# Mixer C's weight chunks: low parts made by accumulating transfers, high passes first, other hand-out rules in the planner

## The chip, the core and the metric

One core of one Trainium2 chip runs the whole program. The metric is the device time of one execution in microseconds (us), the median of the runs shown. TensorE (PE) multiplies, PEld is its weight load, VectorE is DVE, ScalarE is ACT, GpSimd is POOL, and SyncE (SP) issues most transfers from and to the memory off the core (HBM).

## What is computed

Two layers of an encoder over 512 tokens of 1024 channels, in float32. Each layer normalises and modulates its input, projects it once, runs three token mixers on the projections, and merges them by gates:

```python
for l in range(DEPTH):                                   # 2
    shift, scale, gate = jnp.split(c_act @ w_ada[l] + b_ada[l], 3, axis=-1)
    h = rms_norm(x, norm_w[l]) * (1.0 + scale) + shift
    (qa, ka, va, ga, qb, kb, vb, gb, xc, zc, bc, cc, dtf, dtb, mg) = split(h @ w_in[l])
    ya = mixer_a(qa, ka, va, ...) * silu(ga)             # attention, 8 heads
    yb = mixer_b(qb, kb, vb, ...) * silu(gb)             # dilated window attention, 12 heads
    yc = mixer_c(xc, zc, bc, cc, dtf, dtb, ...)          # two-way state space scan, 8 heads
    g_a, g_b, g_c = split(sigmoid(mg + b_gate[l]))
    merged = g_a * (ya @ w_proj_a[l]) + g_b * (yb @ w_proj_b[l]) + g_c * (yc @ w_proj_c[l])
    x = x + gate * (merged @ w_out[l])
```

## The kernel before

**Products.** Every float32 product is made of three passes in a reduced float32 format: an operand is split into a high part (rounded to that format) and a low part (the operand less its high part), and PE adds high·high, high·low and low·high. Weights come as chunks of 128 rows by 1024 columns (512 KB) from the tensor `wch`. `chunk` (line 527) loads one into a `wraw` buffer by a transfer issued from SP, rounds it into a `whi` buffer on ACT, and subtracts on DVE into a `wlo` buffer (line 535); there are three buffers of each. `mm` (line 549) walks a chunk's row blocks k and for each calls `mm_k` (line 539): two passes with the high block, one with the low block, before it goes to the next k. A projection of 8 row blocks (`proj`, line 559) is 24 matmuls of 512 columns.

**The order of work.** The program is first only recorded: each call on an engine becomes an operation with its tiles (`Rec.record`, line 228). A list scheduler (`schedule`, line 306) then plays the machine through with costs written in the code, takes at each moment the ready operation of the lowest priority number per engine, hands out tile buffers as it goes, and issues all in the order found. So an engine's queue order is fixed before the run, and an instruction in it waits in line behind those ahead of it. What steers the order: `AHEAD` (line 464) moves a chunk's loading and splitting that many operations ahead of its use; `RESERVE` (line 457) says how many buffers of a kind must stay free when an operation takes one out of turn (kinds not named there are never given out of turn); `patience` (line 218) and `wait` (line 219) are thresholds in nanoseconds and in shares of an operation's cost, for an operation whose port is taken by the other of DVE and POOL, and for giving way to urgent operations. Some operations are recorded for either of two engines, and the planner chooses.

**A layer.** `record` (line 1369) goes through mixer A, mixer B and mixer C, then the projection of C's branch, then the output projection `out` (line 1309), which for the first layer runs over into the next layer's normalisation. Work without a mixer of its own is kept in a list `fill` and is let in by `pump` at set places. In mixer C (`mixer_c`, line 1172) these are the 8 projections of branch A (`branch_steps`, line 1279), and of branch B the 8 gates (`gate_step`, line 1266) and 8 projections: 16 fill steps, let in after the heads (`PLAN["c"]`). So while mixer C is recorded, `chunk` is called 26 times in a layer: 12 of mixer C's own, 4 for branch A's projection, 8 for branch B's gates and 2 for its projection. A head of mixer C (`ssd_head`, line 1224) is four pairs of scans on DVE over rows in PSUM, sums and products of these on POOL or DVE, a split into parts on ACT and POOL or DVE, and 8 matmuls. Ahead of the heads `steps` (line 1092) makes the step sizes by some 40 small operations on DVE, one after the other, and behind them `tok_rms` (line 739) makes the norm that the branch needs.

**Where the stages lie in the profiled run** (us from the start): start of layer 0 until 82; its mixer A until 200 and mixer B until about 365; entry to mixer C 365 to 380, mixer C 380 to 545, its norm 545 to 563; branch C and output 563 to 643; turn to layer 1 643 to 680. Layer 1: mixer A until 835, mixer B until about 1003, mixer C 1003 to 1172, its norm until 1185, the rest until 1283.

Of the kernel before, what the change touches and what calls it, by code (L numbers as in the profile page):

```python
# [7 lines left out]
F32 = mybir.dt.float32  # L8
F32R = mybir.dt.float32r
I32 = mybir.dt.int32  # L10
AF = mybir.ActivationFunctionType
ALU = mybir.AluOpType
# [195 lines left out]
class Rec:  # L208
# [6 lines left out]
    hold = None  # L215
    urgent = False
    margin = 200
    patience = 0
    wait = 0.4

    def tile(self, tag, shape, dt=F32, psum=False):
        return V(Tl(tag, shape, dt, psum))
# [5 lines left out]
    def record(self, alts):  # L228
        op = Op()
        op.i = len(self.ops)  # L230
        op.prio = op.i + self.boost
        op.alts = {}
        op.dma = 0
        op.urgent = self.urgent and alts[0][1] != "dma_start"
        for eng, meth, args, kw in alts:
            kw = dict(kw)
            if meth == "matmul":
                kw["lhsT"], kw["rhs"] = args[1], args[2]
            out = kw.get("out", args[0] if args else None)
            writes = [out] if isinstance(out, V) else []  # L240
            if isinstance(kw.get("accum_out"), V):
                writes.append(kw["accum_out"])
            reads = [a for a in args[1:] if isinstance(a, V)] + \
                    [v for k, v in kw.items() if isinstance(v, V) and k not in ("out", "accum_out")]
            n = out.n if isinstance(out, V) else 1
            ptr = sum(1 for v in reads if v.n == 1 and n > 1)
            if meth == "dma_start":
                v = out if isinstance(out, V) else reads[0]
                op.dma = v.n * v.p * 4
                inside = all(isinstance(z, V) and not z.t.tag.startswith("dram") for z in (out, *reads))  # L250
                op.slow = 2 if inside and reads else 1
                c = (600 if eng == "sync" else 950, 0, False)
            elif eng == "tensor":
                c = cost_pe(meth, kw, args) + (False,)
            elif eng == "vector":
                if meth == "tensor_reduce":
                    n = reads[0].n
                c = cost_dve(meth, out, reads, ptr, "accum_out" in kw, n)
            elif eng == "scalar":
                c = cost_act(meth, out, reads, ptr, "accum_out" in kw, n)  # L260
            else:
                c = cost_pool(meth, out, reads, ptr, n)
            if meth == "matmul":
                kw.pop("lhsT"), kw.pop("rhs")
            op.alts[ENG[eng]] = (c[0], eng, meth, args, kw, c[1], c[2])
        deps = {}
        pe = eng == "tensor"
        for v in reads:
            for o, box, w in v.t.log:
                if w and self.meet(box, v.box):  # L270
                    deps[o] = 0
        for v in writes:
            if pe and v.t.psum and v.t.lastpe is not None:
                deps.setdefault(v.t.lastpe, 0)
            for o, box, w in v.t.log:
                if o is not op and self.meet(box, v.box) and not (pe and "PE" in o.alts):
                    deps[o] = 0
        for v in writes:
            if pe and v.t.psum:
                v.t.lastpe = op  # L280
            v.t.log = [e for e in v.t.log if not self.inside(e[1], v.box)] + [(op, v.box, True)]
        for v in reads:
            v.t.log.append((op, v.box, False))
        op.tiles = list({id(v.t): v.t for v in reads + writes}.values())
        for t in op.tiles:
            if t.left == 0:
                t.seq = len(self.tags.setdefault(t.tag, []))
                self.tags[t.tag].append(t)
            t.left += 1
        deps.pop(op, None)  # L290
        if meth == "dma_start" and self.hold is not None:
            deps.setdefault(self.hold, -2000)
        op.deps = deps
        op.succ = []
        self.ops.append(op)
        return op
# [157 lines left out]

class Kernel:
    SLOTS = {"wraw": 3, "whi": 3, "wlo": 3, "h": 16, "xs": 7, "gate": 3, "merged": 8, "tmp": 6, "P": 3, "bias": 1, "u4": 12, "q": 4, "s1": 32, "sm": 8, "dt": 2, "wa": 1}
    RESERVE = {"u4": 5, "tmp": 2, "sm": 3, "s1": 9, "ps_mm": 1, "ps_tp": 0, "wraw": 0, "q": 1, "ps_pv": 3}
    BYTES = {"wraw": 4096, "whi": 4096, "wlo": 4096, "u4": 4096, "P": 3072, "bias": 10240, "s1": 32, "sm": 256, "dt": 256,
             "dtr": 256, "dt96": 384}
    START = ("mm", "mm", "sc", "sc", "pv", "pv")  # L460
    POOLADA = ()
    ADAPE = (8, 9, 10)
    POOLLO = ()
    AHEAD = 1114
    WA = "wraw"
    START_W = (2, 3, 4, 5, 6, 6, 6, 6)
    URGENT, URGENT_ROWS = 2, False
    ROWS = ("sc", "sc")
    SOON = 100
    ADATAGS = ("whi", "wlo")  # L470
    PLAN = {"a": 5, "c": (5, 1, 1, 2, 2, 0, 4, 1)}
    BANKS = {"mm": 2, "sc": 2, "tp": 2, "pv": 2}

    def __init__(self, nc, tc, A, depth=DEPTH, dbg=None):
# [52 lines left out]
    def chunk(self, l, j, tags=("wraw", "whi", "wlo"), ahead=None, pool=False):  # L527
        nc = self.nc
        b, self.rec.boost = self.rec.boost, self.rec.boost - (self.AHEAD if ahead is None else ahead)
        raw = self.t(tags[0], [128, 1024])  # L530
        nc.sync.dma_start(raw, self.A["wch"][l, j])
        hi = self.t(tags[1], [128, 1024], F32R)
        nc.scalar.copy(hi, raw)
        lo = self.t(tags[2], [128, 1024], F32R)
        self.sub(lo, raw, hi.bitcast(F32), pool)
        self.rec.boost = b
        return hi, lo

# [8 lines left out]
        nc.tensor.matmul(ps, lo[:, c], xh, start=False, stop=(k == nk - 1), **kw)  # L547

    def mm(self, ps, w, c0, nk, xs):
        for k in range(nk):  # L550
            self.mm_k(ps, w, c0, k, nk, xs)

    def soon(self, f):

# [617 lines left out]
    def mixer_c(self, l):  # L1172
# [7 lines left out]
        for g in range(2):  # L1180
# [10 lines left out]
            for ti in range(2):  # L1191
# [4 lines left out]
                for s in range(2):  # L1196
                    po.append(self.ssd_head(2 * ct + s, s, X, cb, R, d8))
                    self.pump(self.PLAN["c"][2 * ct + s])
                y = self.gather_heads(po[0], po[1], False)
# [63 lines left out]
        return o  # L1263


    def gate_step(self, l, br, n):

        m = 8 * br + n
        ps = self.proj(l, CH_MG + m)
        if br == 0:  # L1270
            g = self.t("merged", [128, 512])
            self.merged.append(g)
        else:
            g = self.t("gate", [128, 512])
        self.soon(lambda: self.nc.scalar.activation(g, ps, AF.Tanh, scale=0.5,
                                                    bias=self.vec[l][:, V_BGATE + m:V_BGATE + m + 1]))
        return g

    def branch_steps(self, l, br, ys, gates=None):

        nk = len(ys)
        per = 8 // nk
        st = {}

        def step(n):
            nc = self.nc
            g = gates[n] if gates else self.gate_step(l, br, n)
            if n % per == 0:
                st["w"] = self.chunk(l, (CH_PA, CH_PB, CH_PC)[br] + n // per)
            p = self.ps("mm")  # L1290
            self.mm(p, st["w"], (n % per) * nk * 128, nk, lambda k: (ys[k][:, 0], ys[k][:, 1]))
            self.soon(lambda: nc.vector.scalar_tensor_tensor(g, g, 1.0, p, op0=ALU.add, op1=ALU.mult))
            if br:
                a = (self.merged[n], self.merged[n], g)
                self.rec.either(("vector", "tensor_add", a, {}), ("gpsimd", "tensor_add", a, {}))

        return [lambda n=n: step(n) for n in range(8)]
# [70 lines left out]

    def record(self):
        self.early = {}  # L1370
        self.xd = [self.dram([128, 512]) for _ in range(8)]
        self.setup()
        for l in range(self.depth):
            if l == 0:
# [22 lines left out]
                    self.early[l, z] = pss[z]  # L1397
                self.bias_vd = self.bias_rows(*self.bias_loads())
                self.setup2()
            self.bg = [(l, o) for o in range(16, 24)] + ([(l + 1, o) for o in range(16)] if l + 1 < self.depth else [])  # L1400
            self.merged = []
            n0 = self.PLAN["a"]
            self.fill = [lambda n=n: self.gate_step(l, 0, n) for n in range(n0)]
            ya = self.mixer_a(l)
            self.pump(8)
            yb = [self.mixer_b(l, jj) for jj in range(2)]
            st0 = self.branch_steps(l, 0, ya, self.merged)
            if n0 < 8:
                self.fill = [lambda n=n: self.gate_step(l, 0, n) for n in range(n0, 8)]
                self.pump(8)  # L1410
            self.fill = st0 + self.branch_steps(l, 1, yb)
            yc = self.mixer_c(l)
            self.pump(16)
            self.tick(24)
            self.fill = self.branch_steps(l, 2, yc)
            self.pump(8)
            self.out(l)

    def prepare(self):
# [2 lines left out]
    def build(self):  # L1422
        from contextlib import ExitStack
        nc, tc, rec = self.real_nc, self.tc, self.rec
        self.record()
        order = rec.schedule(self.RESERVE)
        self.order = order
# [149 lines left out]
```

## Time and profile before

| | before |
|---|---|
| median of 3 runs | 1284.81 us (1283.31 to 1287.2) |
| the profiled execution's own time | 1284.8 us |
| its span, first to last instruction | 1282.9 us |
| PE busy | 1229.2 us (96%), 6288 matmuls |
| DVE busy | 1018.6 us (79%) |
| ACT, POOL busy | 668.5 us (52%), 227.2 us (18%) |
| granted TensorE clock, mean | 0.989 |

Matmuls overlap in the profile: a matmul of 512 columns stands as some 0.39 us long while the next begins 0.23 us after it. So PE's busy time in a stretch tells when PE had nothing in flight, and the granted clock tells where it ran at half its speed; a difference of either from full is time in which PE could have done more. The other engines' busy times can be read as they stand. Every operation is issued from one helper line (L452), so groups are told apart by their tiles: `ps_mm<-h,wlo` is a projection's low pass, `wlo<-wraw,whi` the making of a chunk's low part.

### The profile page before, as it was taken

The page shows a single profiled execution, that of the slowest core. Times are in us where ns is not written, and L with a number is a line of the kernel's source. Part 1 is how long each engine was busy: PE and PEld are TensorE (multiplying, and loading weights), DVE is VectorE, ACT ScalarE, POOL GpSimd, SP SyncE. Part 2 cuts the span into 40 slices and gives each one's busy share as a digit, 9 for nine tenths or more (in the row PEclk, how much of TensorE's full clock was granted, in tenths as well). Part 3 has the DMA queues.
Part 4 walks back from the last instruction along what each step waited for, and adds up shares of the span by engine and source line. Part 5 has one row for each costly group of instructions (what it writes and reads, how often), then busy time and mean ns, then how long its engine had stood idle before and what let it go on. Part 6 is the DMA issues. An engine that isn't in the chain of part 4 may idle for free.

```text
span 1282.9 us, 17593 instructions
## 1 busy us (share of the span) xinstructions
PE 1229.2 (96%) x6288; PEld 1009.2 (79%) x6288; DVE 1018.6 (79%) x1876; ACT 668.5 (52%) x1138; POOL 227.2 (18%) x230
## 2 busy tenths in 40 slices
PE   6999999999989999999989999999999899999998
PEld 5778888788768777778887888887888777777887
DVE  7869977888799999964685889486787999998542
ACT  3447764665554555433344667556665454644320
POOL 0122110210024425300002121001101232442000
PEclk9999999999989999999989999999999998999999
DMA  9643215655312222333643331263342122222341
GB/s 356 212 119 114 66 55 170 179 168 191 89 50 66 66 66 83 99 106 124 213 132 90 108 99 34 83 187 109 95 138 75 53 80 66 66 82 83 123 148 58
DMA packets 49237, 144.32 MB, mean 112 GB/s; under 512 B 7254, under 2 KB 9814, under 8 KB 49150
## 3 DMA queue, kind: packets, MB, share of 16 engines
q1 hardware_dynamic: 49054, 143.07, 35.9%
q8 instruction: 50, 0.82, 0.3%
q14 instruction: 37, 0.30, 0.1%
q0 software_dynamic: 96, 0.13, 0.0%
HBM read 124.74 MB, written 4.27 MB: 101 GB/s over the span
## 4 chain that ended last, share of the span: by engine, by line
PE 76%; DVE 11%; DMA 6%; ACT 3%; issue 2%; SPq 1%; POOL 0%; DVEq 0%; ACTq 0%; POOLq 0%
PE ps_mm L452 55%; PE ps_sc L452 8%; PE ps_tp L452 7%; PE ps_pv L452 7%; DVE wlo L452 3%; DMA wraw<-in_wada 2%; DMA u<-u 2%; DVE u L452 2%; DVE xs L452 1%; DVE tmp L452 1%; DVE P L452 1%; ACT whi L452 1%; DVE q L452 1%; DMA wraw<-in_wch 1%; SPq L452 1%
## 5 line engine op out<-in xcount | busy, mean ns | idle before, releaser
L452 PE MATMUL ps_mm<-h,whi 128*128 128x512 f32 x1824 | 593.3, 396 | 4.3 <-ACT gate L452 3.9
L452 PEld LDWEIGHTS ps_mm<-h,whi 128*128 128x128 f32 x1824 | 340.0, 189 | 79.4 <-ACT gate L452 8.6
L452 PE MATMUL ps_mm<-h,wlo 128*128 128x512 f32 x912 | 359.8, 395 | 0.0
L452 ACT CAST whi<-wraw 128x1024 fp32r<-128x1024 f32 x157 | 164.8, 1051 | 197.7 <-PE ps_mm L452 186.3
L452 DVE TENSOR_TENSOR wlo<-wraw,whi 128x1024 fp32r<-128x1024 f32 x157 | 200.7, 1279 | 71.9 <-ACT whi L452 70.1
L452 PEld LDWEIGHTS ps_mm<-h,wlo 128*128 128x128 f32 x912 | 172.0, 189 | 35.6
L452 PE MATMUL ps_mm<-u,whi 128*128 128x512 f32 (+1 forms) x592 | 177.1, 379 | 16.2 <-DVE merged L452 15.3
L452 PEld LDWEIGHTS ps_mm<-u,whi 128*128 128x128 f32 x592 | 109.5, 192 | 38.5 <-DVE merged L452 17.3
L452 PE MATMUL ps_mm<-u,wlo 128*128 128x512 f32 (+1 forms) x296 | 111.0, 375 | 0.0
L452 PE MATMUL ps_pv<-u,u 128*128 128x256 f32 (+2 forms) x640 | 105.7, 291 | 4.1 <-ACT gate L452 2.8
L452 POOL TENSOR_SCALAR P<-P,s 128x512 f32<-128x512 f32 (+1 forms) x59 | 52.1, 887 | 319.0 <-DVE s L452 251.5
L452 DVE TENSOR_TENSOR u<-ps_tp,u 128x512 fp32r<-128x512 f32 (+2 forms) x174 | 82.7, 489 | 25.8 <-ACT u L452 24.5
L452 DVE TENSOR_TENSOR_SCAN P<-ps_sc,bias 128x512 f32<-128x512 f32 (+3 forms) x128 | 97.6, 803 | 1.6 <-PE ps_sc L452 1.4
L452 ACT CAST u<-ps_tp 128x512 fp32r<-128x512 f32 (+2 forms) x174 | 72.5, 428 | 49.5 <-PE ps_tp L452 44.9
L452 PEld LDWEIGHTS ps_pv<-u,u 128*128 128x128 f32 (+1 forms) x640 | 81.2, 173 | 15.7 <-ACT gate L452 3.0
L452 PE MATMUL ps_sc<-u,q 128*128 128x256 f32 (+1 forms) x320 | 82.9, 361 | 3.4 <-DMA u<-u 2.7
L452 PE MATMUL ps_tp<-const,P 128*128 128x128 f32 x448 | 68.9, 274 | 1.3 <-DVE sm L452 0.7
L452 ACT ACTIVATE bias<-const,dt 128x128 f32<-128x128 f32 x102 | 39.1, 400 | 54.8 <-DVE P L452 50.6
L452 PEld LDWEIGHTS ps_tp<-const,P 128*128 128x128 f32 x448 | 52.9, 140 | 16.4 <-issue 5.6
L452 PEld LDWEIGHTS ps_mm<-u,wlo 128*128 128x128 f32 x296 | 56.8, 192 | 9.8
L452 PEld LDWEIGHTS ps_sc<-u,q 128*128 128x128 f32 x320 | 51.6, 189 | 15.0 <-DMA u<-u 4.1
L452 POOL TENSOR_TENSOR tmp<-tmp,tmp 128x512 fp32r<-128x512 f32 (+1 forms) x15 | 20.6, 1375 | 215.1 <-ACT tmp L452 215.1
(168 smaller groups left out, 1811.2 us busy)
## 6 DMA issues: line engine op xcount, KB each, us to landing
wraw<-in_wch SPq DMA_DIRECT2D x168, 512.0 KB, 3.6
wraw<-in_wada SPq DMA_DIRECT2D x32, 512.0 KB, 3.5
u<-u SPq DMA_DIRECT2D x28, 256.0 KB, 3.7
merged<-in_xT SPq DMA_DIRECT2D x16, 256.0 KB, 3.3
whi<-in_wada SPq DMA_DIRECT2D x8, 512.0 KB, 7.0
wlo<-in_wada SPq DMA_DIRECT2D x8, 512.0 KB, 7.1
u<-u SPq DMA_DIRECT2D x64, 64.0 KB, 2.1
tmp<-xs SPq DMA_DIRECT2D x40, 64.0 KB, 2.7
```

Source lines behind the costliest of these rows:

```text
L452: getattr(getattr(nc, eng), meth)(*[get(a) for a in args], **{k: get(v) for k, v in kw.items()})
```

## The change

1. In `chunk`, while `self.adds` is set and the buffer is of the kind `wlo`: ACT writes the negative of the rounded chunk into `wlo` (an activation with scale -1), POOL issues a transfer that adds the same chunk from HBM onto it, and ACT makes `whi` after that. The subtraction on DVE goes. `self.adds` is set only while mixer C is recorded (`ADDS[0]`): 26 chunks in a layer, 52 in all; the other 4 places are off.
2. The planner counts an accumulating transfer at twice the bytes (`op.slow = 2`).
3. `mm` makes all high passes of a chunk's blocks first and then all low passes. `mm_k` is left for the callers that use it directly (the start and the turn between the layers).
4. `RESERVE`: u4 5 to 2, sm 3 to 2, ps_mm 1 to 0, ps_pv 3 to 1, gate and xs newly named with 1 and 2 (all looser); ps_tp 0 to 1, q 1 to 2 (tighter). `AHEAD` 1114 to 800, `patience` 0 to 300, `wait` 0.4 to 0.2.
5. `PLAN["g"]` is 0, so the list of gates `gc` stays empty, and `pump(24)` finds the same 16 steps as before.

```diff
@@ Rec
-    patience = 0
-    wait = 0.4
+    patience = 300
+    wait = 0.2
@@ record
-                op.slow = 2 if inside and reads else 1
+                op.slow = 2 if inside and reads or "accum_op" in kw else 1
@@ Kernel
-    RESERVE = {"u4": 5, "tmp": 2, "sm": 3, "s1": 9, "ps_mm": 1, "ps_tp": 0, "wraw": 0, "q": 1, "ps_pv": 3}
+    RESERVE = {"u4": 2, "tmp": 2, "sm": 2, "s1": 9, "ps_mm": 0, "ps_tp": 1, "wraw": 0, "q": 2, "ps_pv": 1, "gate": 1, "xs": 2}
-    AHEAD = 1114
+    AHEAD = 800
+    ADDS = (True, False, False, False, False)
@@ chunk
         hi = self.t(tags[1], [128, 1024], F32R)
-        nc.scalar.copy(hi, raw)
         lo = self.t(tags[2], [128, 1024], F32R)
-        self.sub(lo, raw, hi.bitcast(F32), pool)
+        if tags[2] == "wlo" and self.adds:
+            nc.scalar.activation(lo, raw, AF.Copy, scale=-1.0)
+            nc.gpsimd.dma_start(lo, self.A["wch"][l, j], accum_op=ALU.add)
+            nc.scalar.copy(hi, raw)
+        else:
+            nc.scalar.copy(hi, raw)
+            self.sub(lo, raw, hi.bitcast(F32), pool)
@@ mm
         for k in range(nk):
-            self.mm_k(ps, w, c0, k, nk, xs)
+            for z, x in enumerate(xs(k)):
+                nc.tensor.matmul(ps, hi[:, c[k]], x, start=(k == 0 and z == 0), stop=False)
+        for k in range(nk):
+            nc.tensor.matmul(ps, lo[:, c[k]], xs(k)[0], start=False, stop=(k == nk - 1))
@@ record of a layer
+            self.adds = self.ADDS[0]
             yc = self.mixer_c(l)
-            self.pump(16)
+            self.pump(24)
             self.tick(24)
+            self.adds = self.ADDS[1]
```

## Rows read from the trace of the kernel before

**Rows 1.** The page's first two parts: engines' shares, and the span in 40 slices.
```profile
PE 1229.2 (96%) x6288; PEld 1009.2 (79%) x6288; DVE 1018.6 (79%) x1876; ACT 668.5 (52%) x1138; POOL 227.2 (18%) x230
DVE  7869977888799999964685889486787999998542
PEclk9999999999989999999989999999999998999999
...
GB/s 356 212 119 114 66 55 170 179 168 191 89 50 66 66 66 83 99 106 124 213 132 90 108 99 34 83 187 109 95 138 75 53 80 66 66 82 83 123 148 58
```
**Rows 2.** Table by stretch: us, busy (count) of five engines, PEclk, DMA share, GB/s.
```profile
82.00:200.00 118.00, 117.83 (x640) 97.67 (x640) 102.96 (x191) 77.61 (x153) 23.08 (x22) 1.00 0.30 91
245.00:335.00 90.00, 89.02 (x527) 73.45 (x526) 75.87 (x175) 59.05 (x103) 11.24 (x9) 1.00 0.51 156
...
680.00:835.00 155.00, 152.25 (x809) 125.23 (x808) 117.42 (x203) 95.86 (x181) 25.61 (x28) 1.00 0.28 86
870.00:960.00 90.00, 89.41 (x532) 75.04 (x531) 66.10 (x153) 58.46 (x101) 10.28 (x10) 1.00 0.39 110
```
**Rows 3.** The same table, the six stretches around the two mixers C.
```profile
365.00:380.00 15.00, 9.83 (x59) 8.12 (x59) 14.87 (x37) 7.21 (x14) 2.33 (x3) 0.89 0.23 70
380.00:545.00 165.00, 159.31 (x684) 125.96 (x683) 158.83 (x230) 83.09 (x133) 64.03 (x70) 0.99 0.24 74
545.00:563.00 18.00, 16.22 (x69) 13.08 (x70) 11.00 (x25) 5.08 (x9) 0.00 (x0) 0.91 0.19 58
...
1003.00:1005.00 2.00, 1.05 (x5) 0.55 (x3) 2.00 (x4) 0.27 (x1) 0.00 (x0) 1.00 0.02 2
1005.00:1172.00 167.00, 157.46 (x666) 124.18 (x667) 157.96 (x236) 84.97 (x137) 63.07 (x57) 0.97 0.23 73
1172.00:1185.00 13.00, 11.14 (x55) 8.78 (x54) 10.67 (x24) 5.28 (x8) 0.00 (x0) 1.00 0.28 81
```
**Rows 4.** Groups by shape, DVE, 380 to 545: count | busy us, mean ns | idle before.
```profile
L452 DVE TENSOR_TENSOR wlo<-wraw,whi 128x1024 fp32r<-128x1024 f32 x23 | 32.4, 1413 | 0.3
L452 DVE TENSOR_TENSOR_SCAN P<-ps_sc,bias 128x512 f32<-128x512 f32 x16 | 19.2, 1198 | 0.0
...
L452 DVE TENSOR_SCALAR xs<-tmp,const 128x512 f32<-128x512 f32 x5 | 3.5, 700 | 0.0
```
**Rows 5.** The page's part 5: a chunk's parts, and projections' low passes on PE.
```profile
L452 PE MATMUL ps_mm<-h,wlo 128*128 128x512 f32 x912 | 359.8, 395 | 0.0
L452 ACT CAST whi<-wraw 128x1024 fp32r<-128x1024 f32 x157 | 164.8, 1051 | 197.7 <-PE ps_mm L452 186.3
L452 DVE TENSOR_TENSOR wlo<-wraw,whi 128x1024 fp32r<-128x1024 f32 x157 | 200.7, 1279 | 71.9 <-ACT whi L452 70.1
```
**Rows 6.** Timelines of DVE and PE at the entries: start, us, [idle before].
```profile
373.14 1.23 DVE L452 TENSOR_TENSOR wlo<-wraw,whi 128x1024 fp32r<-128x1024 f32 x1
...
376.68 1.28 DVE L452 SCALAR_TENSOR_TENSOR merged<-merged,ps_mm 128x512 f32<-128x512 f32 x2
...
377.42 0.79 PE L452 MATMUL ps_mm<-u,whi 128*128 128x512 f32 x1 [5.17 <-DVE merged L452]
...
1006.88 0.50 PE L452 MATMUL ps_mm<-u,whi 128*128 128x512 f32 x1 [2.83 <-DVE merged L452]
```
**Rows 7.** Chain that ended last: one stretch of projections, and behind layer 1's mixer C.
```profile
435.40 5.68 PE ps_mm L452 x25
...
1170.93 1.06 ACT whi L452
1172.01 1.22 DVE wlo L452
1173.27 0.71 DVE tmp L452
```
**Rows 8.** The page's part 6, transfers by issue: KB each, median us to landing.
```profile
wraw<-in_wch SPq DMA_DIRECT2D x168, 512.0 KB, 3.6
whi<-in_wada SPq DMA_DIRECT2D x8, 512.0 KB, 7.0
const<-in_ident POOLq DMA_DIRECT2D x1, 64.0 KB, 3.6
```
**Rows 9.** POOL's timeline at the start: start, us, one issue of a transfer.
```profile
1.27 0.76 POOL L452 DMA_DIRECT2D const<-in_vec  x1 [0.83 <-POOLq L1569]
```

More of the change, by code (lines that the diff above doesn't have):

```diff
@@ L470 @@
     ADATAGS = ("whi", "wlo")
-    PLAN = {"a": 5, "c": (5, 1, 1, 2, 2, 0, 4, 1)}
+    ADDS = (True, False, False, False, False)
+    PLAN = {"a": 5, "c": (5, 1, 1, 2, 2, 0, 4, 1), "g": 0}
     BANKS = {"mm": 2, "sc": 2, "tp": 2, "pv": 2}
@@ L549, in mm @@
     def mm(self, ps, w, c0, nk, xs):
+        nc = self.nc
+        hi, lo = w
+        c = [slice(c0 + k * 128, c0 + k * 128 + 128) for k in range(nk)]
         for k in range(nk):
-            self.mm_k(ps, w, c0, k, nk, xs)
+            for z, x in enumerate(xs(k)):
+                nc.tensor.matmul(ps, hi[:, c[k]], x, start=(k == 0 and z == 0), stop=False)
+        for k in range(nk):
+            nc.tensor.matmul(ps, lo[:, c[k]], xs(k)[0], start=False, stop=(k == nk - 1))
     def soon(self, f):
@@ L1263, in ssd_head, with gate_step @@
         return o
-    def gate_step(self, l, br, n):
+    def gate_step(self, l, br, n, tag="gate"):
         m = 8 * br + n
@@ L1273, in gate_step @@
         else:
-            g = self.t("gate", [128, 512])
+            g = self.t(tag, [128, 512])
         self.soon(lambda: self.nc.scalar.activation(g, ps, AF.Tanh, scale=0.5,
@@ L1286, in step @@
             nc = self.nc
-            g = gates[n] if gates else self.gate_step(l, br, n)
+            g = gates[n] if gates and n < len(gates) else self.gate_step(l, br, n)
             if n % per == 0:
@@ L1370, in record @@
         self.early = {}
+        self.adds = False
         self.xd = [self.dram([128, 512]) for _ in range(8)]
@@ L1399, in record @@
                 self.setup2()
+            self.adds = self.ADDS[3]
             self.bg = [(l, o) for o in range(16, 24)] + ([(l + 1, o) for o in range(16)] if l + 1 < self.depth else [])
@@ L1405, in record @@
             self.pump(8)
+            self.adds = self.ADDS[4]
             yb = [self.mixer_b(l, jj) for jj in range(2)]
@@ L1410, in record @@
                 self.pump(8)
+            gc = []
             self.fill = st0 + self.branch_steps(l, 1, yb)
+            self.fill += [lambda n=n: gc.append(self.gate_step(l, 2, n, "xs")) for n in range(self.PLAN["g"])]
+            self.adds = self.ADDS[0]
             yc = self.mixer_c(l)
-            self.pump(16)
+            self.pump(24)
             self.tick(24)
-            self.fill = self.branch_steps(l, 2, yc)
+            self.adds = self.ADDS[1]
+            self.fill = self.branch_steps(l, 2, yc, gc)
             self.pump(8)
+            self.adds = self.ADDS[2]
             self.out(l)
```

## Prediction

> **What bounds the kernel now.** I read the page's first two parts, then a table of busy times by stretch, then the groups of the stretch that stood out, and last the timeline where PE waits. PE is busy 96% of the span, so at first sight PE is the bound everywhere and a change on DVE can bring nothing [rows 1]. The slices tell more: DVE stands at 9 in two places, the two mixers C, and the granted clock drops from 9 to 8 near their ends [rows 1].
>
> The table by stretch makes it exact. In the mixers A and B of both layers PE idles 0.17 of 118 us, 0.98 of 90, 2.75 of 155 and 0.59 of 90, at full clock, with DVE busy 87%, 84%, 76% and 73% [rows 2]. That is 4.5 us of 453, or 1.0%: PE is the bound there, and a DVE at up to 87% does not hold it up. In the two mixers C DVE is busy 158.83 of 165 us and 157.96 of 167, or 96% and 95%, and PE idles 5.69 and 9.54 us [rows 3]. At the entry to layer 0's mixer C DVE is busy 14.87 of 15 us and PE idles 5.17 [rows 3]. So around the mixers C both are near full, DVE more so, and PE loses time to it.
>
> What is lost there: PE's idle time in the six stretches is 5.17 + 5.69 + 1.78 + 0.95 + 9.54 + 1.86 = 25.0 us [rows 3]. To it comes the clock. The granted share is 0.89 of 15 us, 0.99 of 165, 0.91 of 18 and 0.97 of 167, so 1.65 + 1.65 + 1.62 + 5.01 = 9.9 us of full-speed work is missing [rows 3]; each drop to the lower level, 1.2 instead of 2.4 GHz, follows a wait of PE. Together 34.9 us. More than that this change cannot win around mixer C.
>
> **The subtraction that goes.** 26 chunks per layer leave DVE. One subtraction takes 1.28 us in the mean over the kernel [rows 5] and 1.41 us in layer 0's mixer C [rows 4]; it is the largest group of DVE there, with 32.4 us for the 23 that fall into the stretch [rows 4]. 26 x 1.28 = 33 us a layer. DVE falls from 158.8 to about 126 us. If the stretch shrinks to some 156 us, that is 81%, which lies between the 73% and 87% at which PE was not held up [rows 2]. So DVE stops being the bound, and PE is next.
>
> **What stays lost.** (a) PE's own small waits at the rate of the other stages: 1.0% of the 380 us of the six stretches, 3.8 us [rows 2, 3]. (b) The norm behind mixer C is a chain of small dependent steps, in which PE lost 1.78 + 1.62 + 1.86 = 5.3 us [rows 3]. In the chain of layer 1 one subtraction of 1.22 us stands ahead of it on DVE [rows 7]; without one in each layer 2.8 us stay. (c) At the entries PE waits for DVE to empty a PSUM bank, 5.17 and 2.83 us [rows 6]. In the longer wait DVE works through its queue, of which one subtraction is only 1.23 us [rows 6]; the rest are the small operations of `steps` and others. With the clock of the first entry (1.65) 9.65 us are lost; I keep half, 4.8, since the queue ahead is shorter but the serial steps remain. 3.8 + 2.8 + 4.8 = 11.4 stay, and 34.9 - 11.4 = 23.5 us are won.
>
> **What is added.** ACT gets one more pass of 1.05 us per chunk [rows 5], 27 us a layer, and stands then at 83 + 27 = 110 of some 156 us (70%) [rows 3]; the same ACT also turns conv and gate outputs over, but at 70% it hides that. The high part is ready one pass later, and is loaded well ahead: PE waited 0.0 us ahead of the low passes [rows 5]. If that cover were gone, each chunk would cost up to 1.05 us.
>
> POOL gets 26 issues a layer. Nearest row: 0.76 us for an issue from POOL [rows 9]; 20 us, so POOL goes from 64 to 84 of 156 us [rows 3]. Each issue waits for ACT's negation, and behind it on POOL are the sums and products of the heads' scans, on which the heads' matmuls wait. Bounds: nothing, if the planner places the issue after the negation, to 26 x 1.05 = 27 us a layer, if POOL stands through one whole ACT pass each time and nothing else is ready. I take 1 us a layer, near the lower end, since POOL idles 101 of 165 us now [rows 3]. Together 2.
>
> The transfer itself: no row shows one that accumulates. A plain 512 KB chunk from SP lands after 3.6 us, under the load of the start after 7.0, a 64 KB one from POOL after 3.6 [rows 8]. Bounds 3.6 and, at the planner's factor of two on the longest, 14 us; I take 8, twice the plain one and a little for the load: 26 chunks of 0.52 MB are 13.6 MB a layer, 27 at twice their bytes; with the 12 MB that 74 GB/s move in 165 us [rows 3] that is 39 MB in 156 us, or 250 GB/s, 70% of the 356 seen in the first slice [rows 1]. So no lasting queue of transfers forms, but it is no longer a quiet stretch. SP's own queue gets nothing new; its loads wait for a free `wraw`, which ACT's second pass now frees instead of DVE.
>
> **High passes first.** The low part is wanted only after 16 of a chunk's 24 matmuls. A matmul takes 5.68 / 25 = 0.227 us [rows 7], so 3.6 us later: nearly half of the landing is hidden by that alone, the rest by loading ahead. The number of matmuls and weight loads is the same. What it costs: the last block's operand is wanted 7 matmuls sooner (15th instead of 22nd), at most 1.6 us where it is fresh. That is so only at the first output chunk of a layer; I take half, 0.8, twice, 1.6 us.
>
> **The planner's other numbers** (`RESERVE`, `AHEAD`, `patience`, `wait`) reorder all stages and no row prices them. The nearest measure is how far two orders of the same code differ: mixer A loses 0.17 of 118 us in one layer and 2.75 of 155 in the other [rows 2], 0.1% against 1.8%. 1.7% of the 453 us of these stages is 7.7 us, to either side; I take 0, as neither sign has a reason.
>
> **Sum.** 23.5 - 2 - 1.6 = 19.9 us. The profiled execution took 1284.8 us with a span of 1282.9, and is at the median of the runs (1284.81), so no further shift is due: 1284.8 - 19.9 = **1265 us**, 1.5% faster. Its own range: all 34.9 won and 4 of the 7.7, 1246; the 7.7 against it and 6 more for POOL, 1279.
>
> **A rule against it.** DVE's single-input elementwise form in this stretch is only five instructions of 3.5 us in all [rows 4]. The Trainium skill, SBUF — State Buffer, SBUF: two separate sides, says that a transfer issued from GpSimd has its descriptors written by GpSimd, and that a DVE instruction that takes both port pairs locks it out until it ends, so that the transfer looks blocked. By that rule five landings of 26 would come under 1 us later; the sum stays, and it adds to the chance of the second rival.
>
> **The rivals.** *No change:* the heads' own chain, scans on DVE, sums on POOL, split on ACT, matmuls, is the bound by its length, and PE waits as before; 1281 to 1288, say 1285. For it: ACT and POOL wait much for DVE's scans. Against: DVE has no gaps, its groups show 0.0 to 0.3 us idle [rows 4], so it lacks time, not input. 0.12.
>
> *The accumulating transfer lands late:* slower. A low buffer is held from the negation to its last low pass: 1.05 + 0.76 + landing + 8 x 0.227 = landing + 3.6 us. Three buffers serve 26 chunks in 165 us if this is under 3 x 6.35 = 19 us. So the point is a landing of 15.4 us; beyond it PE waits for chunks. At 18 us: 26 x 21.6 / 3 = 187 us, 22 more a layer, 1329 us. Against it: every 512 KB landing seen, 7.0 at most [rows 8]. Starved descriptors would be its cause. 0.09.
>
> *POOL's queue stands:* slower. POOL has 165 - 84 = 81 us to spare, so 3.1 us of standing per issue. At 4 us each POOL takes 64 + 26 x 4.76 = 188 us, 23 more a layer, 1331. Against it: the planner sees the negation's end before it places the issue. 0.09.
>
> **How the numbers follow.** Forecast 0.70, no change 0.12, late transfer 0.09, POOL 0.09. What a measurement can tell is 0.3%, 3.9 us: 1281 to 1288.7 is the same. Of the forecast's 0.70 about 0.02 falls there, and of the no-change rival's 0.12 about 0.03 on the faster side and 0.01 on the slower. Faster 0.71, same 0.10, slower 0.19. The range goes from the forecast's best end, 1246, over no change to 1288; 0.16 to 0.18 of the slower cases and a little below stay out.
>
> **What would show it.** Right: DVE in mixer C's stretch at 75 to 85%, no `wlo<-wraw,whi` there; the stretches from the entry to the norm's end shorter by 8 to 13 us in each layer, other stages within some us; the drops of the clock after the entries fewer; landings of the accumulating transfers of 4 to 9 us, and none named as what PE waits for. Wrong: PE's low passes waiting for a transfer or POOL; POOL's waits for ACT grown by over 80 us a layer; gains or losses that lie in the mixers A and B, which would make the planner's numbers the cause.

## The result, and the profile after

| | before | after |
|---|---|---|
| median | 1285.12 us (1283.31 to 1287.2) | 1262.58 us (1261.5 to 1268.03) |
| the profiled execution's own time | 1284.8 us | 1262.41 us |
| its span | 1282.9 us | 1260.6 us |
| granted TensorE clock, mean | 0.989 | 0.996 |

Both kernels ran on the same chip, four times each. The time after is 0.9833 of the time before, 95% interval 0.9801 to 0.9865: 22.5 us faster, where 19.9 were forecast.

The page of after: shares of the engines, the slices of DVE, POOL and the granted clock, and the groups and transfers of a low part (count | busy us, mean ns | idle before; KB and median us to landing):

```profile
PE 1222.3 (97%) x6288; PEld 1006.8 (80%) x6288; DVE 962.0 (76%) x1747; ACT 726.8 (58%) x1202; POOL 374.8 (30%) x347
...
DVE  7869966888698979864685899586767999897442
...
POOL 0033310020136858611014221001002385682110
PEclk9999999999999999999999999999999999999999
...
L452 POOL DMA_DIRECT2D wlo<-in_wch x52 | 46.2, 889 | 172.9 <-ACT wlo L452 153.3
...
wraw<-in_wch SPq DMA_DIRECT2D x168, 512.0 KB, 3.8
wlo<-in_wch POOLq DMA_DIRECT2D x52, 512.0 KB, 6.5
```

The clock's three eights of [rows 1] are gone (they stood at the entry to layer 0's mixer C, at the turn and at the end of layer 1's mixer C). But DVE still reaches 9 in slices of both mixers C, and POOL, busy 64.03 of 165 us in layer 0's mixer C before [rows 3], has slices of 5 to 8 in both. DVE has 129 instructions fewer. Only 52 of these are the subtractions, worth 52 x 1.28 = 67 us [rows 5]; the other 77 went to other engines in the new plan: POOL has 117 instructions more, 52 of them the issues, and ACT has 64 more, 52 of them the negations, which leaves 65 + 12. For all this DVE's busy time fell by 56.6 us only: what stayed on DVE became longer.

The table by stretch of after (us, busy (count) of PE, PEld, DVE, ACT, POOL, then the granted clock, DMA share, GB/s): entry to layer 0's mixer C, the mixer, its norm; the turn; the end of layer 1's mixer B, its mixer C, its norm. They answer to [rows 3].

```profile
365.00:377.00 12.00, 11.98 (x84) 10.08 (x83) 11.45 (x37) 8.83 (x22) 6.62 (x7) 1.00 0.73 154
377.00:530.00 153.00, 147.28 (x639) 117.43 (x639) 137.00 (x187) 102.96 (x158) 112.63 (x104) 0.99 0.63 141
530.00:550.00 20.00, 20.00 (x96) 16.58 (x95) 14.73 (x29) 8.83 (x12) 1.28 (x1) 1.00 0.25 79
630.00:670.00 40.00, 37.67 (x298) 36.04 (x297) 27.66 (x67) 18.50 (x35) 5.99 (x7) 1.00 0.33 106
...
945.00:986.00 41.00, 38.95 (x228) 31.73 (x227) 33.59 (x103) 28.40 (x61) 11.85 (x12) 0.96 0.53 117
986.00:1144.00 158.00, 150.04 (x669) 119.86 (x667) 145.66 (x192) 105.80 (x165) 106.52 (x103) 1.00 0.62 138
1144.00:1162.00 18.00, 17.82 (x84) 14.20 (x83) 14.32 (x29) 8.46 (x12) 0.00 (x0) 1.00 0.27 87
```

And the turn of before, which [rows 3] leave out:

```profile
643.00:680.00 37.00, 31.56 (x247) 31.36 (x248) 26.79 (x70) 15.15 (x28) 0.00 (x0) 0.91 0.36 114
```

Counted as in the prediction (PE's idle time plus the missing share of the clock), the stretches from the entry to the norm lost 34.9 us before. Now they lose 0.02 + (5.72 + 1.53) + 0 + 7.96 + 0.18 = 15.4 us: 19.5 won. The turn lost 5.44 + 3.33 = 8.8 and loses 2.3, 6.4 more won. Against that the end of layer 1's mixer B now loses 2.05 + 1.64 = 3.7 us, where before PE was busy 43.00 of 43 us (960 to 1003). These three make 22.2 of the 22.4 us between the two profiled executions; smaller shifts at the start and in layer 1's mixer A cancel within about 1.5 us.

What PE waits for after in layer 0's mixer C, then the longest wait in layer 1's (us in total, times, longest us), and what POOL waits for in the two:

```profile
PE ps_pv L452 <- ACT u L452: 3.5, 2, 2.4
PE ps_mm L452 <- ACT gate L452: 1.2, 3, 0.5
PE ps_pv L452 <- DVE u L452: 0.9, 1, 0.9
```
```profile
PE ps_tp L452 <- DVE xs L452: 3.1, 1, 3.1
```
```profile
POOL wlo L452 <- ACT wlo L452: 19.1, 12, 5.4
```
```profile
POOL wlo L452 <- ACT wlo L452: 34.8, 12, 7.8
```

No transfer is named for PE. In layer 0 what is late now is mostly the operand of the heads' own matmuls (`ps_pv`), split by ACT and DVE: the chain of the first rival, behind the forecast's bound. In layer 1 the longest single wait is for a result of DVE, `xs`.

### The profile page after: what moved, and what is told of

It is laid out like the page before. It is cut to its first block, busy times and chain, and to the rows that moved or that the text cites. A ratio compares the mean times of both kernels' runs of the same rounds, so it can differ in the third digit from the quotient of the medians.

```text
span 1260.6 us, 17709 instructions
## 1 busy us (share of the span) xinstructions
PE 1222.3 (97%) x6288; PEld 1006.8 (80%) x6288; DVE 962.0 (76%) x1747; ACT 726.8 (58%) x1202; POOL 374.8 (30%) x347
## 5 line engine op out<-in xcount | busy, mean ns | idle before, releaser
L452 PE MATMUL ps_mm<-h,whi 128*128 128x512 f32 x1824 | 476.6, 396 | 5.3 <-ACT gate L452 3.5
L452 PE MATMUL ps_mm<-h,wlo 128*128 128x512 f32 x912 | 244.2, 393 | 0.0
L452 DVE TENSOR_TENSOR wlo<-wraw,whi 128x1024 fp32r<-128x1024 f32 x105 | 136.9, 1305 | 79.0 <-PE ps_mm L452 47.9
L452 PE MATMUL ps_mm<-u,whi 128*128 128x512 f32 (+1 forms) x592 | 141.2, 375 | 0.3 <-ACT gate L452 0.2
L452 PEld LDWEIGHTS ps_mm<-u,whi 128*128 128x128 f32 x592 | 104.2, 188 | 20.6 <-ACT gate L452 0.6
L452 DVE TENSOR_TENSOR u<-ps_tp,u 128x512 fp32r<-128x512 f32 (+2 forms) x174 | 83.2, 490 | 21.4 <-ACT u L452 20.6
L452 POOL DMA_DIRECT2D wlo<-in_wch x52 | 46.2, 889 | 172.9 <-ACT wlo L452 153.3
L452 POOL TENSOR_TENSOR tmp<-tmp,tmp 128x512 fp32r<-128x512 f32 (+1 forms) x23 | 35.0, 1523 | 189.9 <-ACT tmp L452 186.4
L452 POOL TENSOR_TENSOR u<-P,u 128x384 f32<-128x384 f32 (+3 forms) x76 | 77.7, 1071 | 3.9 <-DVE P L452 3.2
L452 PE MATMUL ps_mm<-u,wlo 128*128 128x512 f32 (+1 forms) x296 | 74.7, 374 | 0.0
L452 POOL TENSOR_TENSOR merged<-merged,gate 128x512 f32<-128x512 f32 x20 | 37.4, 1874 | 123.3 <-DVE gate L452 123.1
L452 POOL TENSOR_TENSOR u<-u,u 128x1024 fp32r<-128x1024 f32 x27 | 69.4, 2570 | 9.8 <-ACT u L452 9.8
```

The costliest lines, as they stand in the source:

```text
L452: getattr(getattr(nc, eng), meth)(*[get(a) for a in args], **{k: get(v) for k, v in kw.items()})
```

## The experiments

Two kinds were run. In the first, parts of the change are set back and the planner makes a new order. In the second, called *in place*, the planned order of a kernel is kept and only the instruction issued at a place is exchanged, so nothing moves but what is named. Each ratio is against the kernel before on the same chip (its median 1283.1 to 1285.6 us).

| kernel | transfers add | high first | planner's numbers | median us | ratio [95%] |
|---|---|---|---|---|---|
| adds_only | yes | no | old | 1304.73 | 1.0142 [1.0101, 1.0183] |
| adds_high_first (in place) | yes | yes | old | 1284.77 | 0.9994 [0.9972, 1.0015] |
| old_numbers | yes | yes | old | 1287.26 | 1.0022 [1.0000, 1.0044] |
| old_reserve | yes | yes | `RESERVE` old | 1283.23 | 0.9986 [0.9962, 1.0010] |
| old_ahead | yes | yes | `AHEAD` old | 1264.01 | 0.9825 [0.9799, 0.9852] |
| old_order | yes | no | new | 1328.54 | 1.0336 [1.0305, 1.0368] |
| no_adds | no | yes | new | 1290.74 | 1.0050 [1.0029, 1.0071] |
| high_first_in_place | no | yes | old | 1284.25 | 0.9988 [0.9961, 1.0015] |
| after | yes | yes | new | 1262.58 | 0.9833 [0.9801, 0.9865] |

### Is the subtraction on DVE what bound mixer C?

**no_adds**: after with the subtraction on DVE again, planned anew.

```diff
-    ADDS = (True, False, False, False, False)
+    ADDS = (False, False, False, False, False)
```

> The changed kernel with all low parts made on DVE again. If the subtraction is what gains: 1275 to 1288, with DVE at 95% in mixer C as before. If the planner's numbers and the order of passes gain: 1262 to 1270.

28 us slower than after, and 0.5% slower than before: without the transfers the other two parts bring nothing. The time is just above the expected 1288, and DVE is not at 95% over the whole mixers: from 380 to 545 it is busy 149.16 us, 90%, no more than in after. PE's loss lies at the ends of the two mixers, and there DVE is at 93% and 95%:

```profile
500.00:542.00 42.00, 31.92 (x109) 22.84 (x108) 39.04 (x49) 19.52 (x31) 35.69 (x30) 0.76 0.16 52
...
1130.00:1160.00 30.00, 18.55 (x60) 12.54 (x59) 28.46 (x36) 13.13 (x23) 24.76 (x20) 0.71 0.12 36
```

PE loses 20.2 + 20.2 = 40 us in these 72. Of DVE, ACT and POOL the first is the busiest there, but the named waits of PE go to POOL and ACT for `u` as well, and few other matmuls run in these ends (109 in 42 us, 60 in 30).

**sub_in_place**: after's order; the 52 negations and transfers are left out, and DVE subtracts where the negation and the high part are both ready.

```diff
+            a = nc.scalar.activation(lo, raw, AF.Copy, scale=-1.0)
+            d = nc.gpsimd.dma_start(lo, self.A["wch"][l, j], accum_op=ALU.add)
+            h = nc.scalar.copy(hi, raw)
+            self.rec.skip |= {a.i, d.i}
+            self.rec.subs[h.i] = self.rec.subs[a.i] = [0, (lo, raw, hi.bitcast(F32))]
```

> The changed kernel with its order of instructions kept as planned, but in each of the 52 chunks the negation on ACT and the transfer from POOL are left out and the subtraction is put back on DVE, at the place where the high part is ready. If the freed DVE is what gains: 1275 to 1290 us and DVE at 95% or more in mixer C. If the new order as such gains and DVE's time is not short: 1258 to 1266.

1304.91 us, 1.0158 [1.0134, 1.0181]: 42 us slower than after and above the expected 1290, although ACT and POOL have less to do. Its two mixers C, by the table by stretch:

```profile
377.00:552.00 175.00, 156.03 (x673) 120.55 (x672) 167.87 (x212) 87.33 (x144) 101.57 (x87) 0.98 0.22 67
986.00:1180.00 194.00, 172.45 (x774) 135.10 (x773) 183.99 (x287) 99.50 (x174) 99.50 (x88) 0.99 0.22 66
```

DVE is back at 96% and 95%, and PE's idle time there goes from 5.7 and 8.0 to 19.0 and 21.6 us. So in after's order the mechanism of the forecast holds: with the subtraction on it, DVE's time is what is short. Its worth is 28 us where the plan may adapt and 42 where it may not; some of the 42 may belong to an order that was not planned for the subtraction.

### Does the transfer arrive late, and what hides it?

**adds_only**: the transfers put into the kernel before, nothing else changed, planned anew.

```diff
+        if tags[2] == "wlo" and self.adds:
+            nc.scalar.activation(lo, raw, AF.Copy, scale=-1.0)
+            nc.gpsimd.dma_start(lo, self.A["wch"][l, j], accum_op=ALU.add)
+            nc.scalar.copy(hi, raw)
```

> The kernel before with the accumulating transfers alone (low pass after each block's high passes, planner's numbers as before). If the subtraction that leaves DVE is what gains, as the prediction had it: 1262 to 1272 us, DVE in mixer C well under 95%. If the hand-out numbers are what gains: 1280 to 1290. If the landing of 6.5 us needs the high passes first to hide it: 1275 or more, with PE waiting for the transfer ahead of low passes.

About 20 us slower than before. PE's longest waits of the whole run:

```profile
PE ps_mm L452 <- ACT gate L452: 8.9, 10, 1.5
PE ps_mm L452 <- DMA wlo<-in_wch: 8.0, 8, 1.8
PE ps_mm L452 <- DVE merged L452: 6.3, 3, 5.0
```

The second line is the second rival, at a landing of 6.9 us, far under the 15.4 from which the prediction let it count.

**adds_high_first**: the order planned for adds_only kept; inside 180 of 183 products the passes change places, the high ones first.

```diff
+        self.rec.groups.append((g, [o for n, o in enumerate(g) if n % 3 < 2] + g[2::3]))
```

> The kernel with the accumulating transfers alone (1304.7 us), its planned order kept, but with the high passes moved first, in place, in 180 of the 183 chunk products. If the high passes hide the landing: PE no longer waits for the transfers (8.0 us in 8 waits before) and the time falls by 8 to 20 us, to 1285 to 1297. If the loss of that kernel is in the planned order and not in the landing: 1300 to 1306.

20 us faster than adds_only (1304.73 to 1284.77) with the same landing:

```profile
wlo<-in_wch POOLq DMA_DIRECT2D x52, 512.0 KB, 6.9
```

No wait of PE for it is left among its longest. The 20 us are more than the 8.0 us of named waits; where the other 12 lie was not told apart.

This run also shows that DVE's relief alone does not bring the gain. It has the transfers and the high passes first, only the planner's numbers are old, and it takes as long as before. Its two mixers C:

```profile
380.00:545.00 165.00, 155.17 (x673) 122.93 (x671) 142.73 (x215) 102.92 (x158) 76.00 (x81) 0.99 0.62 141
...
1003.00:1172.00 169.00, 159.70 (x682) 127.49 (x683) 146.70 (x224) 106.13 (x160) 79.05 (x72) 0.98 0.64 140
```

DVE stands at 87% in both, the share at which the prediction saw PE not held up, and still PE loses 11.5 + 12.7 = 24.2 us there, no less than the 22.9 before (380 to 545 and 1003 to 1172). What it wins at the entries and norms it loses in the mixers B: 7.1 + 1.7 = 8.7 us from 200 to 365, where before lost 3.8, and 7.8 from 860 to 1003, where before lost 0.6:

```profile
200.00:365.00 165.00, 157.92 (x915) 131.53 (x914) 131.24 (x300) 101.19 (x167) 22.17 (x19) 0.99 0.59 166
860.00:1003.00 143.00, 135.24 (x802) 111.22 (x800) 103.55 (x264) 91.77 (x164) 22.27 (x22) 1.00 0.45 114
```

This order was planned for the old passes; old_numbers below is planned for the new ones, and takes as long.

**high_first_in_place**: the same exchange in the kernel before, in 179 of 183 products.

> The kernel before with its planned order, but within 179 of the 183 chunk products the passes are rearranged so that the high passes come first, at the same places on PE. The prediction held that PE never waits for a low part there: 1282 to 1287, no change. If the low part's lateness costs something unseen: 1270 to 1280.

1284.25 us, 0.9988 [0.9961, 1.0015], no difference beyond some 4 us. So the pass order by itself neither costs nor brings anything that shows; with the transfers it is worth 20 us. The likely reason is that in the old order the low pass of a chunk's first block is wanted at its third matmul.

**old_order**: after with the old pass order, planned anew.

```diff
     def mm(self, ps, w, c0, nk, xs):
         for k in range(nk):
+            self.mm_k(ps, w, c0, k, nk, xs)
```

> The changed kernel with each block's low pass right after its high passes. If the order only hides the landing and loading ahead hides it too: 1260 to 1268, no change. If the order is needed for the transfers: 1270 or more and PE waiting for the transfer or for weights.

66 us slower than after. PE waits for `wlo<-in_wch` 7.8 us, as in adds_only. But its largest single loss lies in layer 1's mixer B, where no such transfer runs. The table by stretch, old_order and then the kernel before:

```profile
903.00:960.00 57.00, 39.65 (x196) 29.66 (x196) 25.39 (x63) 21.02 (x40) 1.82 (x2) 0.70 0.16 44
```
```profile
903.00:960.00 57.00, 56.54 (x350) 48.83 (x349) 44.15 (x104) 34.55 (x59) 5.83 (x6) 1.00 0.42 116
```

PE runs 196 matmuls there instead of 350, at a clock of 0.70: the plan seems to have put little other work beside the attention's chain. It loses 17.4 + 17.1 = 34 us, about half of the whole difference. An edit that is planned anew shows the edit and a new order together; that is why the disputed costs were measured in place.

**plain_in_place**: after's order; the 52 transfers overwrite instead of adding.

```diff
+            if "accum_op" in kw:
+                kw = {}
```

> The changed kernel with the same order, but the 52 transfers from POOL overwrite instead of adding, so that the low parts hold the whole weights. If adding itself costs nothing on the path: 1260 to 1265, with landings of some 4 to 5 us in place of 6.5. If the landing still holds PE up: 1250 to 1258. If landings stay at 6.5, it is the POOL queue or the load and not the adding that sets them.

1256.17 us, 0.9771 [0.9744, 0.9799], 6 us faster than after (0.9833 [0.9801, 0.9865]). One issue on POOL takes 569 ns instead of 889, and the landing 4.6 us instead of 6.5. The page of it, and its first mixer C by the table:

```profile
L454 POOL DMA_DIRECT2D wlo<-in_wch x52 | 29.6, 569 | 179.6 <-ACT wlo L454 159.2
...
wlo<-in_wch POOLq DMA_DIRECT2D x52, 512.0 KB, 4.6
```
```profile
377.00:525.00 148.00, 146.92 (x648) 118.30 (x648) 135.76 (x186) 102.42 (x160) 102.70 (x104) 1.00 0.46 150
```

The adding thus costs about 6 us of time, though PE is never named as waiting for it. Whether by the landing or by the 52 x 0.32 = 17 us of POOL was not told apart.

### Why did DVE stay at 90%?

**pool_writes**: after's order; each of the 27 subtractions of 1024 columns that POOL does for the heads is replaced by three fills of the same tile, which read nothing and take POOL 3.1 us instead of 2.6; these low parts are zeros.

```diff
+                for _ in range(3):
+                    nc.gpsimd.memset(get(args[0]).bitcast(F32), 0.0)
```

> The changed kernel with the same order, but the 1024-element subtractions of the heads that the planner gave to POOL (u from u, u, 2.6 us each, reading SBUF) are three fills of the same buffer, about as long and reading nothing; those low parts are zeros. If POOL's reads are what lengthens DVE's two-input instructions: DVE's busy time in the two mixers C falls by 10 to 25 us in all and the time to 1250 to 1259. If they do not contend: DVE as long as before and 1260 to 1265.

1258.21 us, 0.9795 [0.9772, 0.9819], 4.4 us faster than after, with POOL just as busy; the interval touches that of after, so the 4.4 us are at the edge of what can be told. What is clear is DVE's busy time in the two mixers C, which goes from 137.0 + 145.7 to 129.9 + 128.6 us:

```profile
377.00:528.00 151.00, 148.58 (x665) 117.93 (x663) 129.89 (x191) 104.54 (x161) 113.49 (x129) 1.00 0.65 145
986.00:1142.00 156.00, 151.45 (x659) 120.10 (x658) 128.64 (x189) 105.28 (x165) 111.35 (x132) 1.00 0.64 142
```

**split_on_dve**: after's order; the same 27 subtractions on DVE.

```diff
+            if o.i in self.moved:
+                eng = "vector"
```

> The changed kernel with the same order, but the 1024-element subtractions of the heads' split all on DVE (1.2 us each there, 2.6 on POOL, 27 of 32 on POOL before). If their contention costs DVE as much as they take: DVE's busy time about the same, POOL's less by some 70 us, and 1254 to 1262. If DVE binds mixer C again: 1265 to 1285.

1264.98 us, 0.9834 [0.9806, 0.9861], the same as after, between the two expected ranges. POOL's busy time falls by 65 us and DVE's rises by only 2.6 (962.0 to 964.6), although DVE does 32 of these subtractions instead of 5, 49.4 us instead of 7.8. So POOL's 27 cost DVE, in longer instructions, nearly what they would cost on DVE itself: 39 us by these figures, of which pool_writes, where POOL still writes, gave back 24 in the mixers.

Which instructions get longer is read from three groups of DVE over the whole run (count | busy us, mean ns | idle before): before, after, pool_writes and split_on_dve, whose helper line is numbered differently.

```profile
L452 DVE TENSOR_TENSOR P<-P 128x128 f32<-128x128 f32 x30 | 9.5, 318 | 0.0
L452 DVE TENSOR_SCALAR xs<-tmp,const 128x512 f32<-128x512 f32 x16 | 9.4, 586 | 0.0
L452 DVE TENSOR_TENSOR q<-tmp,gate 128x512 f32<-128x512 f32 x8 | 5.5, 684 | 0.0
```
```profile
L452 DVE TENSOR_SCALAR xs<-tmp,const 128x512 f32<-128x512 f32 x16 | 16.1, 1004 | 2.1 <-ACT tmp L452 2.1
L452 DVE TENSOR_TENSOR P<-P 128x128 f32<-128x128 f32 x21 | 12.7, 606 | 0.1
L452 DVE TENSOR_TENSOR q<-tmp,gate 128x512 f32<-128x512 f32 x8 | 8.7, 1091 | 0.1
```
```profile
L457 DVE TENSOR_SCALAR xs<-tmp,const 128x512 f32<-128x512 f32 x16 | 18.7, 1170 | 4.1 <-ACT tmp L457 4.1
L457 DVE TENSOR_TENSOR P<-P 128x128 f32<-128x128 f32 x21 | 10.3, 491 | 0.1
L457 DVE TENSOR_TENSOR q<-tmp,gate 128x512 f32<-128x512 f32 x8 | 5.4, 678 | 0.1
```
```profile
L455 DVE TENSOR_SCALAR xs<-tmp,const 128x512 f32<-128x512 f32 x16 | 12.2, 761 | 2.1 <-ACT tmp L455 2.0
L455 DVE TENSOR_TENSOR P<-P 128x128 f32<-128x128 f32 x21 | 7.0, 333 | 0.0
L455 DVE TENSOR_TENSOR q<-tmp,gate 128x512 f32<-128x512 f32 x8 | 5.4, 676 | 0.1
```

The product `q<-tmp,gate` with two inputs goes from 684 to 1091 ns, and is back at 678 and 676 as soon as POOL's large subtractions no longer read; the sum `P<-P` goes from 318 to 606 and falls to 491 and 333. The operation with one tensor as input, `xs<-tmp,const`, goes from 586 to 1004, gets no better with the fills in place of the reads (1170), and falls where POOL does less (761). One stretch of pool_writes shows it directly: of four two-input operations at 0.68 us each, the first three run while POOL fills (start, us):

```profile
446.31 2.71 DVE L457 SCALAR_TENSOR_TENSOR xs<-tmp,const,xs 128x511 f32<-128x511 f32 x4
```
```profile
445.15 3.13 POOL L455 MEMSET u<- 128x1024 f32 x3
```

Not every two-input group falls: `xs<-xs,tmp` goes from 684 to 1027 ns and stays at 1009 in pool_writes. POOL's other operations read in that kernel as before, and may be what holds it.

The scans, whose one input lies in PSUM, stay: 1198 ns before [rows 4], and after, in layer 0's mixer C:

```profile
L452 DVE TENSOR_TENSOR_SCAN P<-ps_sc,bias 128x512 f32<-128x512 f32 x16 | 19.3, 1205 | 0.3 <-POOL u L452 0.3
```

The Trainium skill, SBUF — State Buffer, Who interferes with whom, says the same: a DVE instruction with two inputs in SBUF contends with a GpSimd instruction that reads SBUF and not with one that only writes it, while the two-port form of a one-input instruction contends with GpSimd at large. In the three groups above the four kernels agree; that `xs<-tmp,const` takes the two-port form they do not show by themselves.

### Which of the planner's numbers matters?

**old_numbers**, **old_reserve** and **old_ahead**: after with all numbers of before, with `RESERVE` alone, with `AHEAD` alone set back, each planned anew.

```diff
-    RESERVE = {"u4": 2, "tmp": 2, "sm": 2, "s1": 9, "ps_mm": 0, "ps_tp": 1, "wraw": 0, "q": 2, "ps_pv": 1, "gate": 1, "xs": 2}
+    RESERVE = {"u4": 5, "tmp": 2, "sm": 3, "s1": 9, "ps_mm": 1, "ps_tp": 0, "wraw": 0, "q": 1, "ps_pv": 3}
...
-    AHEAD = 800
+    AHEAD = 1114
```

> The changed kernel with the planner's numbers of before (hand-out, reach ahead, patience, wait). If the numbers are worth nothing, as the prediction took it: 1258 to 1270. If the looser hand-out carries the gain: 1275 to 1290.

> The changed kernel with the hand-out table (RESERVE) of before alone. All three sets of numbers set back gave 1287 us. If the hand-out carries it: 1280 to 1290. If not: 1258 to 1268. The prediction took it as worth nothing within 7.7 us.

> The changed kernel with the reach ahead (AHEAD) of before alone, 1114 in place of 800. If the hand-out carries the numbers' gain: 1258 to 1268. If the reach does: 1280 to 1290.

All back, the gain is gone (1287.26); `AHEAD` back costs nothing (1264.01); `RESERVE` back costs 20.6 us (1283.23), more than half of it in layer 0's mixer B and most of the rest at the turn, here in the table by stretch of old_reserve:

```profile
245.00:365.00 120.00, 112.40 (x638) 92.92 (x637) 87.20 (x210) 74.16 (x126) 17.78 (x17) 0.94 0.50 137
...
640.00:690.00 50.00, 42.97 (x339) 42.77 (x338) 29.27 (x72) 16.88 (x32) 2.61 (x3) 0.90 0.26 85
```

In mixer B it loses 7.6 + 7.2 = 14.8 us, where after loses 2.0 and before about 1.6; at the turn 7.0 + 5.0 = 12.0, where after loses 2.3 and before 8.8. Since before has the same `RESERVE` and does not lose in mixer B, the table has no fixed price of its own. That it decides what work is left beside the attention, and that this depends on the rest of the plan, is likely but not shown. Which entry does it stays open, and `patience` and `wait` alone were not tried.

Together: of the transfers, the pass order and the numbers, each one set back takes the whole gain away. Their prices (28, 66 and 25 us, each planned anew) do not add up to the 22.5 of the change; each holds only with the other two in place, and each comes from one plan.

## Why the prediction was right, and where its steps were not

The sign and the size (1262.6 against 1265) came true, and the mechanism is there: put back on DVE in the same order, the subtraction costs 42 us and fills DVE (sub_in_place). But the sum is not how the time came about. It credits the freed DVE with 23.5 us and the planner's numbers with 0. With the transfers, the new pass order and the old numbers the gain is 0 within 3 us in adds_high_first and none in old_numbers. That the number fits is in good part luck: in these runs the freed DVE paid only under the new numbers, for which the prediction gave no reason either way, and several smaller errors nearly cancel.

- **"DVE stops being the bound", at 81%.** The size failed. DVE stands at 137.00 of 153 us (90%) and 145.66 of 158 (92%), not at 126. The step took the durations of [rows 4] as fixed while POOL went from some 64 us to 112.6 and 106.5. The prediction gave POOL 84; it missed that the plan would also move sums and subtractions from DVE to POOL. pool_writes shows the price of POOL's large reads: 24 us of DVE in the two mixers, some 4 us of time. Nor is a lower share enough: at 87% PE lost as much in adds_high_first.
- **What stays lost, 11.4 us.** The total was 15.4, its parts other ones. The entries keep almost nothing instead of 4.8: no wait like the 5.17 us of [rows 6] is left. The norms keep 0.2 instead of 2.8. The mixers C keep 15.2 instead of the 3.8 for small waits over all six stretches: layer 0's loses 7.25 us now and lost 7.3 before, layer 1's 7.96 after 14.6 (9.54 + 5.01). The 1.0% of mixers A and B was the wrong row for a mixer whose DVE is still at 90%.
- **High passes first.** Mis-sized. The sum has it as a cost of 1.6 us, too small for high_first_in_place to confirm or exclude, and as a cover for nearly half of the landing with the rest left to loading ahead. It is what makes the transfers pay, 20 us by adds_high_first: loading ahead did not cover the landing in adds_only.
- **The transfer itself.** The landing of 8 us measured 6.5, the 250 GB/s measured 141, and no wait for it is named in after. It was held at nothing; plain_in_place prices the adding at 6 us. The rival's condition, three buffers full at a landing of 15.4 us, was not reached, yet PE waited 8.0 us for transfers in adds_only at 6.9. The condition watched the number of buffers, not how late the single low part is.
- **POOL's issues.** 0.89 us each, not 0.76. POOL waits 19.1 us for ACT's negation in layer 0's mixer C, inside the bound of 27, and 34.8 in layer 1's, outside it; both are far over the 1 us taken. That figure was for time lost, and PE is not named as waiting for POOL in either mixer, so these waits are mostly covered.
- **The planner's numbers, 0 with 7.7 to either side.** This is the step that failed most: a term put at nothing because neither sign had a reason, and `RESERVE` alone is worth 20.6 us by old_reserve. How it works beside the transfers stays open. The measure, two layers of one plan, says nothing on how far two plans differ; old_order, with 34 us lost in a mixer it did not touch, does.
- **The signs set out.** A norm without its wait, landings within 4 to 9 us in the median and none waited for: as written. Three subtractions stand at the end of layer 0's mixer C (521 to 531 us) and two at the end of layer 1's, which belong to work outside the 52 chunks. DVE at 75 to 85% did not come. From the entry to the norm's end 198 us became 185, 13 less, but in layer 1 182 became 176, under the 8 set out. The gain at the turn, 6.4 us, was not foreseen.
- **The rule set against it.** By the Trainium skill, SBUF — State Buffer, SBUF: two separate sides, DVE's two-port instructions would hold back the transfers' descriptors. In layer 0's mixer C the landings are 5.7 us at least, 6.5 in the median and 7.8 at most, so here the spread leaves at most some 2 us for it, and none that PE waits for. The prediction counted five one-input operations before in that stretch; a longer one, `s<-const` of 2.2 us, and a small `sm` stand there too.

## What to carry to other kernels

Work taken off a full engine is worth its time only if what takes its place does not slow that engine: here POOL, made busier, gave some of DVE's other instructions up to about twice their length (`P<-P`, 318 to 606 ns). A transfer that makes an operand late pays only together with an order that wants this operand late; measured one by one, each of the two looks useless or harmful, and here both together brought nothing until the hand-out rules were changed as well. A forecast that comes true in size is not yet explained by its sum. Where a planner orders the whole program, exchange instructions in a fixed order to price one edit, and read a newly planned run as edit plus new plan.

## What the runs showed of the hardware

- A 512 KB transfer that adds lands 6.5 us after its issue from POOL, one that overwrites 4.6, with 52 of them in the same places of the same order; a plain one from SP takes 3.8 in after. While the adding ones run, the DMA engines are busy for 0.63 of the time at 141 GB/s, with the overwriting ones 0.46 at 150.
- The issue of an adding transfer holds POOL for 889 ns, of an overwriting one for 569.
- POOL's large reads lengthen two-input instructions of DVE (`q<-tmp,gate`, 684 to 1091 ns in the mean), fills in their place do not (678); the one-input `xs<-tmp,const` is long with both (586 to 1004 and 1170 ns).
